# Finishing the last MLP product of a two-layer block in token blocks, with resident weights and a running final norm

## The chip, the cores and the metric

The program runs on all eight cores of one Trainium2 chip. The cores do the same work on different tokens and do not communicate. The time of a run is the device time of the slowest core, in microseconds (us). The program has a second, slower state in some executions: a run of the kernel before that took 1701.93 us is one of them. A ratio of two kernels is the mean time of one kernel's fast runs over that of the other's fast runs of the same rounds, so it is not quite the ratio of the medians.

Names: PE is the matmul engine (TensorE), PEld its weight loads, DVE is VectorE, ACT is ScalarE, POOL is GpSimd, SP is SyncE, which here only issues stores and waits. An engine with a "q" behind its name (SPq, POOLq) is its instruction sequencer.

## The reference, cut to what matters

The model is a two-layer block over latent tokens. Each layer mixes tokens and then applies a squared-ReLU MLP. The whole study is about the last two lines of work: the second MLP product of the second layer, and the final norm.

```python
def rmsnorm(x, g):
    xf = x.astype(jnp.float32)
    y = xf * lax.rsqrt(jnp.mean(xf * xf, axis=-1, keepdims=True) + EPS)
    return (y * g.astype(jnp.float32)).astype(x.dtype)

def sq_relu_mlp(h, w1, w2):
    return jnp.square(jax.nn.relu(h @ w1)) @ w2
# ... for each layer:
        x = x + g2 * sq_relu_mlp(h, mlp_w1[i], mlp_w2[i])
# ...
    return rmsnorm(x, final_g)
```

There are 16,384 latent tokens, 2,048 for each core. D_MODEL is 1024, so a token's output has eight chunks of 128 features; the hidden width is 4096. On the chip the features lie on the 128 partitions and the tokens along the free dimension.

## The kernel before

The tokens of a core are four tiles of 512. The MLP works on two tiles at once, so the last product covers the last 1,024 tokens. For each output chunk `fo`, 32 matmuls accumulate over the hidden features for each tile, then DVE adds the result to the residual:

```python
    def mlp_2(st):
        l, g = st["l"], st["g"]
        for fo in range(NCH):
            bks = [P.bank() for _ in st["pieces"]]
            for hf in range(2):
                w = w_take(("w2", l, g, 2 * fo + hf)).rearrange("p (a b) -> p a b", a=16)
                for ti, tile in enumerate(st["pieces"]):
                    # ... 16 matmuls of N = 512 columns into bks[ti]; after hf == 1:
                            P.stt(xv[:, fo, :], bk[:, o:o + n], MOD[:, l, 40 + fo, col:col + 1], xv[:, fo, :], ALU.mult, ALU.add)
```

The final norm needs the mean square over all eight chunks. It is a matmul with a matrix of 1/1024 over the squares (the statistics matmuls), then Ln and Exp on ACT; DVE multiplies each chunk by `final_g` and the factor, and each pair of chunks is stored:

```python
        def fin(c):
            P.stt(xv[:, c, :], xv[:, c, :], GVEC[:, 4, c:c + 1], rs, ALU.mult, ALU.mult)
            if c % 2 == 1:
                outs.append(P.dma("sp", d_out[:, c - 1:c + 1, t * 512:(t + 1) * 512], xv[:, c - 1:c + 1, :]))
        return [(lambda i=i: norm_sq(tiles[t], sqv(SQF, 512), i, 4)) for i in range(4)] + \
               [lambda: norm_stat(sqv(SQF, 512), 512, rs)] + [(lambda c=c: fin(c)) for c in range(NCH)]
    # ...
    run_all(mlp_2(l1[1]))
    for t in (2, 3):
        for f in fin_pieces(t):
            f()
    S.op("sp", None, extra_deps=outs)      # SP waits for all stores
```

All operations pass through a list scheduler in the program (class `Sched`), which fixes each engine's order before the kernel is built and derives the semaphore waits.

The softmax here doesn't subtract the row's maximum and nothing guards it: scores larger than these inputs give would overflow.

Of the kernel before, what the change touches and what calls it, by code (L numbers as in the profile page):

```python
# [13 lines left out]
NCH = 8  # L14
# [12 lines left out]


class _Op:
    __slots__ = ("id", "eng", "chan", "fn", "deps", "signal", "waits", "pos", "inc", "sigval", "cost", "mode", "unit", "prio")  # L30


class Sched:
# [7 lines left out]
    def __init__(self, nc):  # L41
        self.nc = nc
        self.ops = []
        self.streams = {k: [] for k in ("pe", "act", "dve", "pool", "sp")}
        self.chan_ops = {}
        self.buckets = {}
        self.base = {}
        self.hold, self.boost = None, 0

    def rects(self, ap):  # L50
        name = ap.tensor.name
# [63 lines left out]

    def op(self, eng, fn, reads=(), writes=(), chan=None, inc=1, extra_deps=(), cost=100.0, mode=None, join=False):
        o = _Op()
        o.cost, o.mode, o.prio = cost, mode, self.boost
        if self.hold is not None and eng == "pe":
            join = self.hold > 0  # L120
            self.hold += 1
        o.unit = join
        o.id = len(self.ops)
        o.eng = eng
        o.chan = chan or eng
        o.fn = fn
        o.inc = inc
        o.signal = chan is not None
        o.waits = []
        o.sigval = 0  # L130
        accs = []
        for ap in reads:
            if ap is None or isinstance(ap, (int, float)):
                continue
            sp, rs = self.rects(ap)
            for r in rs:
                accs.append((sp, r, sp == "ps"))
        for ap in writes:
            sp, rs = self.rects(ap)
            for r in rs:  # L140
                accs.append((sp, r, True))
        o.deps = self._query_insert(o, accs)
        for d in extra_deps:
            o.deps[d.id] = True
        self.ops.append(o)
        self.streams[eng].append(o)
        lst = self.chan_ops.setdefault(o.chan, [])
        lst.append(o)
        o.pos = len(lst)
        return o  # L150
# [22 lines left out]
    def reorder(self):  # L173
        ops = self.ops
        units = {e: [] for e in self.streams}
        unit_of = [None] * len(ops)
        for o in ops:
            lst = units[o.eng]
            if o.unit and lst:
                lst[-1].append(o)  # L180
            else:
                lst.append([o])
            unit_of[o.id] = (o.eng, len(lst) - 1)
        need, succ = {}, {}
        for e, lst in units.items():
            for i, u in enumerate(lst):
                ds = {unit_of[d] for o in u for d in o.deps}
                ds.discard((e, i))
                need[(e, i)] = len(ds)
                for d in ds:  # L190
                    succ.setdefault(d, []).append((e, i))
        end = [0.0] * len(ops)
        free = {e: 0.0 for e in units}
        head = {e: 0 for e in units}
        taken = {e: [False] * len(l) for e, l in units.items()}
        avail = {e: {} for e in units}
        best = {e: None for e in units}
        dma_free, mode = 0.0, None
        order = []

        def virtual(e, i):
            v, acc = 0.0, 0.0
            for o in units[e][i]:
                for d in o.deps:
                    if unit_of[d] != (e, i):
                        t = end[d] + (0.0 if ops[d].chan == e == "pe" else self.SEM) - acc
                        if t > v:
                            v = t
                acc += o.cost
            return v  # L210

        def pick(e):
            lim = head[e] + self.WINDOW[e]
            cand = []
            for i, v in avail[e].items():
                if i < lim:
                    s = max(free[e], v)
                    if e == "pe" and mode is not None and units[e][i][0].mode != mode:
                        s += 100.0
                    cand.append((s, i))  # L220
            if not cand:
                return None
            lo, li = min(cand)
            tol = lo + min(1500.0, max(150.0, 0.5 * sum(o.cost for o in units[e][li])))
            s, i = min(((s, i) for s, i in cand if s <= tol), key=lambda c: c[1] - units[e][c[1]][0].prio)
            return (s, i)

        for k, n in need.items():
            if n == 0:
                avail[k[0]][k[1]] = virtual(*k)  # L230
        left = len(need)
        while left:
            e, b = None, None
            for k in units:
                if best[k] is None and avail[k]:
                    best[k] = pick(k)
                if best[k] is not None and (b is None or best[k][0] < b[0]):
                    e, b = k, best[k]
            s, i = b
            t = s  # L240
            for o in units[e][i]:
                for d in o.deps:
                    if unit_of[d] != (e, i):
                        t = max(t, end[d] + (0.0 if ops[d].chan == e == "pe" else self.SEM))
                if o.chan.startswith("dma:"):
                    dma_free = max(dma_free, t + 0.6 * self.LAT) + o.cost
                    end[o.id] = dma_free + 0.4 * self.LAT
                    t += 540.0 if e == "pool" else 60.0
                else:
                    t += o.cost  # L250
                    end[o.id] = t + (90.0 if e == "pe" else 0.0)
                order.append(o)
            if e == "pe":
                mode = units[e][i][-1].mode
            free[e] = t
            taken[e][i] = True
            del avail[e][i]
            while head[e] < len(taken[e]) and taken[e][head[e]]:
                head[e] += 1
            best[e] = None  # L260
            left -= 1
            for k in succ.get((e, i), ()):
                need[k] -= 1
                if need[k] == 0:
                    avail[k[0]][k[1]] = virtual(*k)
                    best[k[0]] = None
        self.ops_in_order = order
        self.streams = {e: [o for o in order if o.eng == e] for e in self.streams}
        self.chan_ops = {}
        for o in order:  # L270
            lst = self.chan_ops.setdefault(o.chan, [])
            lst.append(o)
            o.pos = len(lst)
# [61 lines left out]
class Prog:  # L335
# [87 lines left out]
    def stt(self, out, in0, scalar, in1, op0, op1):  # L423
        return self.S.op("dve", lambda e: e.scalar_tensor_tensor(out, in0, scalar, in1, op0, op1),  # L424
                         reads=[in0, in1, scalar], writes=[out], cost=self.ew_cost("dve", "stt", out, [in0, in1]))

    def shuf(self, out, in_, mask):
        return self.S.op("dve", lambda e: e.stream_shuffle(out, in_, mask), reads=[in_], writes=[out],  # L428
                         cost=190.0 + 1.05 * self.n_of(out))
# [21 lines left out]
def run_all(gen):  # L451
    for _ in gen:
        pass
# [37 lines left out]
def build():  # L491
# [63 lines left out]
    def rot(key, lst):  # L555
        i = ctr.get(key, 0)
        ctr[key] = i + 1
        return lst[i % len(lst)]
# [52 lines left out]
    def w_take(key):  # L611
        ada_flush()
        while ada_take(ST):
            pass
        nxt = ST.items[ST.pos][0]
        if nxt[0] in extra:
            extra[nxt[0]](*nxt[1:])
        return ST.take(key)
# [7 lines left out]
    def plan_mlp(l, g, rounds1, rounds2, q0={}):  # L626
        ext1 = [("ada", l_, r_, c) for l_, r_ in rounds1 for c in range(4)]
        ext2 = [("ada", l_, r_, c) for l_, r_ in rounds2 for c in range(4)]
        for j in range(16):
            ST.add(("w1", l, g, j), d_w1[l, j])  # L630
            if j % 2 == 1 and ext1:
                k = ext1.pop(0)
                ST.add(k, d_ada[k[1], k[2], k[3]])
        for j in range(16):
            ST.add(("w2", l, g, j), d_w2[l, j // 2, j % 2])
            if j in q0:
                ST.add(("wq0", q0[j]), d_wq[q0[j]])
            if ext2 and j >= 1:
                k = ext2.pop(0)
                ST.add(k, d_ada[k[1], k[2], k[3]])  # L640
        assert not ext1 and not ext2
# [735 lines left out]
    run_all(mlp_a)  # L1377
    spread(mlp_2(l1[0]), st_norm(l1[1], 0) + st_norm(l1[1], 1))
    spread(mlp_1(l1[1]), fin_pieces(0) + fin_pieces(1), 2, 2)
    run_all(mlp_2(l1[1]))  # L1380
    for t in (2, 3):
        for f in fin_pieces(t):
            f()
    S.op("sp", None, extra_deps=outs)
    S.emit()
    return nc
# [116 lines left out]
```

## Time and profile before

| | before |
|---|---|
| fast runs | 1514.5 and 1516.05 us (the other two runs, 1701.93 and 1714.51 us, were slow) |
| spans of the cores in the profiled run | 1505.0 to 1514.3 us |
| PE busy in the slowest core | 1431.5 of 1514.3 us |
| last product, first to last matmul | 110.67 us on each core |
| from there to the last instruction (the tail) | 18.67 us, mean of cores (17.9 to 19.5) |

The first two lines below are of the page of the slowest core: its span, and each engine's busy time with its share of the span.

```profile
span 1514.3 us, 23295 instructions; the slowest of 8 cores (1505.0 to 1514.3 us)
...
PE 1431.5 (95%) x8436; PEld 694.0 (46%) x8436; DVE 600.9 (40%) x1003; ACT 583.2 (39%) x841; POOL 304.5 (20%) x371
```

PE is the bottleneck over the whole. The end is another matter. The next lines are of the timeline of the kernel before: start in us, duration, engine, line, operation, tiles written and read, shape, count of merged instructions, and in brackets the engine's idle time and what ended it. A merged row lasts from its first start to its last end.

```profile
1494.84 0.38 PE L387 MATMUL ps<-hid_175,ring_61 128*128 128x512 bf16 x1
...
1495.05 2.48 PE L387 MATMUL ps<-sqf_176,onesm_46 128*128 128x512 bf16 x10
...
1498.56 10.90 DVE L424 SCALAR_TENSOR_TENSOR xm_55<-xm_55,small_43,rs_63 128x512 f32<-128x512 f32 x16 [2.48 <-ACT rs_63 L397]
...
1500.04 9.86 SPq L447 DMA_DIRECT2D outT<-xm_55  x8
```

The last product matmul ends at 1495.22 us. Most statistics matmuls follow it. DVE's sixteen final multiplies begin at 1498.56 and run for 10.90 us in one row; the eight stores go out as they come. The chain of waits shows the same (start, duration, what; it is followed back from the end):

```profile
1449.89 47.07 PE ps L387 x218
...
1498.36 2.00 ACT sqf_176 L397 x2
...
1502.55 0.70 ACT rs_63 L397
...
1504.07 0.75 DVE xm_55 L424
...
1505.48 3.98 DVE xm_55 L424 x6
```

The end is one long row of DVE work behind a finished PE. Stores follow within a few us.

Two more lines are of the view of the source line that opens the program's block. At the end of the block each engine executes a DRAIN and then all meet at a barrier. The columns are duration min/median/max in ns, then the start of the first and last in us.

```profile
L311 POOLq DRAIN  x1: 8888/8888/8888, 1461.3 to 1461.3; - x1
...
L311 SPq DRAIN  x1: 7/7/7, 1514.1 to 1514.1; - x1
```

POOL's DRAIN takes 8.9 us here, but it begins at 1461.3, with POOL's last weight load, it is over at 1470.1, and nobody waits for it.

### The profile page before, as it was taken

Reading aid. Unit: us, or ns where it says so; the run is one execution under the profiler, and the core shown is the slowest. Engines: PE = TensorE matmul, PEld = TensorE weight load, DVE = VectorE, ACT = ScalarE, POOL = GpSimd, SP = SyncE. Lnnn points to the kernel's source line nnn. Section 1 sums busy time; section 2 is a strip of 40 time slices with the busy share of each in tenths; the row PEclk is TensorE's granted clock in tenths of the full one; section 3 lists DMA queues with packets and bytes.
Section 4 is the critical chain, followed back from the end, with each engine's and each line's share of the span. In section 5 each row is a group of like instructions: output and inputs, shape, how many; then the busy total and the mean of one; then the engine's idle time right before and its main releaser. Section 6 shows DMA issues by size and latency. Waiting matters only on the chain.

```text
span 1514.3 us, 23295 instructions; the slowest of 8 cores (1505.0 to 1514.3 us)
## 1 busy us (share of the span) xinstructions
PE 1431.5 (95%) x8436; PEld 694.0 (46%) x8436; DVE 600.9 (40%) x1003; ACT 583.2 (39%) x841; POOL 304.5 (20%) x371
## 2 busy tenths in 40 slices
PE   1699999999999999999997999899999999999996
PEld 0344445555555555555543334334444444444442
DVE  0177874443221344322248666443443222552003
ACT  2464363335110333323018778774334121432002
POOL 2025400010100010110135666552000000000000
PEclk9999999999999999999998999999999999999998
DMA  9554715545663455664354000400444444663432
GB/s 193 152 126 70 131 28 94 98 84 90 118 113 63 77 89 104 104 108 74 62 94 74 8 2 2 70 2 15 72 82 70 80 74 71 134 130 70 84 56 111
DMA packets 39808, 124.16 MB, mean 82 GB/s; under 512 B 4240, under 2 KB 4624, under 8 KB 39312
## 3 DMA queue, kind: packets, MB, share of 16 engines
q0 software_dynamic: 29504, 102.90, 39.9%
q1 hardware_dynamic: 10192, 19.76, 4.1%
q8 instruction: 70, 1.15, 0.3%
q14 instruction: 42, 0.34, 0.1%
HBM read 217.15 MB, written 8.39 MB: 149 GB/s over the span
## 4 chain that ended last, share of the span: by engine, by line
PE 90%; DMA 3%; DVE 2%; issue 2%; ACT 1%; POOL 1%; SPq 0%; DVEq 0%; ACTq 0%; POOLq 0%
PE ps L387 89%; DMA xm_55<-xT 2%; DMA ring_59<-ada_r 1%; DVE xm_55 L424 0%; SPq L447 0%; DVE tmp_65 L414 0%; ACT xb_68 L397 0%; POOL qt_122 L414 0%; ACT rs_63 L397 0%; DVE tb_129 L414 0%; DVE tb_130 L428 0%; DVE tb_127 L414 0%; POOL dt_75 L414 0%; DVE tb_128 L414 0%; DVE tb_130 L414 0%
## 5 line engine op out<-in xcount | busy, mean ns | idle before, releaser
L424 DVE SCALAR_TENSOR_TENSOR xm_55<-ps,mod_44,xm_55 128x512 f32<-128x512 f32 (+2 forms) x136 | 97.4, 718 | 296.4 <-PE ps L387 296.1
L397 ACT ACTIVATE tmp_64<-ps 128x512 f32<-128x512 f32 (+2 forms) x156 | 84.8, 543 | 213.6 <-PE ps L387 161.8
L397 ACT ACTIVATE tmp_65<-ps 128x512 f32<-128x512 f32 (+2 forms) x157 | 85.3, 544 | 159.5 <-PE ps L387 98.1
L397 ACT ACTIVATE sqf_176<-xm_55 128x1024 bf16<-128x1024 f32 x16 | 16.7, 1053 | 158.9 <-DVE xm_55 L424 156.9
L387 PE MATMUL ps<-xb_68,win_67 128*128 128x512 bf16 (+1 forms) x192 | 50.2, 422 | 10.2 <-ACT xb_68 L397 9.5
L387 PE MATMUL ps<-h_0_98,ring_61 128*128 128x408 bf16 (+3 forms) x336 | 58.9, 335 | 0.0
L387 PE MATMUL ps<-h_0_98,ring_58 128*128 128x384 bf16 (+3 forms) x336 | 58.9, 335 | 0.0
L414 DVE TENSOR_TENSOR tmp_64<-xm_55,rs_63 128x512 f32<-128x512 f32 (+2 forms) x44 | 33.8, 767 | 48.2 <-ACT rs_63 L397 41.9
L397 ACT ACTIVATE rs_63<-ps,epsv_51 128x512 f32<-128x512 f32 (+3 forms) x16 | 10.6, 666 | 105.2 <-PE ps L387 104.9
L387 PE MATMUL ps<-hid_99,ring_61 128*128 128x416 bf16 (+3 forms) x288 | 51.0, 335 | 0.0
L387 PE MATMUL ps<-h_0_98,ring_60 128*128 128x416 bf16 (+3 forms) x288 | 50.5, 335 | 0.0
L387 PE MATMUL ps<-h_0_98,ring_57 128*128 128x416 bf16 (+3 forms) x288 | 50.4, 335 | 0.0
L387 PE MATMUL ps<-h_0_98,ring_59 128*128 128x416 bf16 (+3 forms) x288 | 50.4, 335 | 0.0
L447 POOL DMA_DIRECT2D ring_59<-w_r x27 | 14.3, 531 | 171.8 <-PE ps L387 171.7
L414 DVE TENSOR_TENSOR hid_100<-tmp_64 128x416 bf16<-128x416 f32 (+3 forms) x48 | 27.9, 581 | 43.8 <-ACT tmp_64 L397 43.8
L414 DVE TENSOR_TENSOR hid_99<-tmp_64 128x416 bf16<-128x416 f32 (+3 forms) x48 | 27.9, 581 | 41.2 <-ACT tmp_64 L397 41.1
L387 PEld LDWEIGHTS ps<-h_0_98,ring_61 128*128 128x128 bf16 x336 | 32.5, 97 | 25.1 <-issue 0.6
L387 PEld LDWEIGHTS ps<-h_0_98,ring_58 128*128 128x128 bf16 x336 | 32.4, 98 | 25.0 <-issue 0.8
L447 POOL DMA_DIRECT2D ring_61<-w_r x27 | 14.3, 530 | 143.3 <-PE ps L387 143.1
L414 DVE TENSOR_TENSOR hid_99<-tmp_65 128x416 bf16<-128x416 f32 (+3 forms) x48 | 27.9, 581 | 37.7 <-ACT tmp_65 L397 37.7
L414 DVE TENSOR_TENSOR hid_100<-tmp_65 128x416 bf16<-128x416 f32 (+3 forms) x48 | 27.9, 581 | 36.0 <-ACT tmp_65 L397 36.0
L447 POOL DMA_DIRECT2D ring_60<-w_r x24 | 12.7, 530 | 138.4 <-PE ps L387 103.7
(803 smaller groups left out, 3136.9 us busy)
## 6 DMA issues: line engine op xcount, KB each, us to landing
ring_61<-w_r POOLq DMA_DIRECT2D x27, 512.0 KB, 5.7
ring_59<-w_r POOLq DMA_DIRECT2D x27, 512.0 KB, 5.8
ring_58<-w_r POOLq DMA_DIRECT2D x26, 512.0 KB, 5.8
ring_57<-w_r POOLq DMA_DIRECT2D x24, 512.0 KB, 5.8
ring_60<-w_r POOLq DMA_DIRECT2D x24, 512.0 KB, 5.9
outT<-xm_55 SPq DMA_DIRECT2D x16, 512.0 KB, 4.9
xm_55<-xT SPq DMA_DIRECT2D x6, 1024.0 KB, 9.0
ring_58<-ada_r POOLq DMA_DIRECT2D x12, 512.0 KB, 5.2
```

The source lines that it names most:

```text
L387: return self.S.op("pe", lambda e: e.matmul(out, lhsT, rhs, start=start, stop=stop), reads=[lhsT, rhs], writes=[out], cost=max(30.0 if hal ...
L397: return self.S.op("act", lambda e: e.activation(out, in_, func, bias=bias, scale=scale), reads=[in_, scale, bias], writes=[out], cost=175 ...
L414: return self.S.op(eng, lambda e: e.tensor_tensor(out, in0, in1, op), reads=[in0, in1], writes=[out], cost=self.ew_cost(eng, "tt", out, [i ...
L424: return self.S.op("dve", lambda e: e.scalar_tensor_tensor(out, in0, scalar, in1, op0, op1), reads=[in0, in1, scalar], writes=[out], cost= ...
L447: return self.S.op(q, lambda e: e.dma_start(out=out, in_=in_), reads=[in_], writes=[out], chan="dma:" + slot, inc=16, extra_deps=dep, cost ...
```

## The change

The intent: let most of the final norm, multiplies and stores run under matmuls. The first four output chunks are computed for all 1,024 tokens as before. The other four are computed for 768 tokens, and then, at the very end, for the last 256 tokens, with the eight weight pieces still resident. While PE does those last 128 matmuls, the other engines finish the 768 tokens. The squares go into the statistics chunk by chunk, so that the norm is ready soon after the last chunk. Two of the last block's eight multiplies go to POOL and ACT, and the stores alternate between the SP and ACT queues.

```diff
@@ plan_mlp
-            ST.add(("w2", l, g, j), d_w2[l, j // 2, j % 2])
+            if (l, g) != (1, 1) or j < 12:
+                ST.add(("w2", l, g, j), d_w2[l, j // 2, j % 2])
@@ the end of build()
-    run_all(mlp_2(l1[1]))
-    for t in (2, 3):
-        for f in fin_pieces(t):
-            f()
     ...
+    blocks = [(0, 0, 512, P.bk(7)[:, 0:512], RS[0][:, 0:512]), (1, 0, 256, P.bk(6)[:, 0:256], RS[1][:, 0:256]),
+              (1, 256, 512, P.bk(5)[:, 0:256], RS[1][:, 256:512])]
     ...
+    for j in range(12, 16):            # into buffers that are dead by now
+        w2_of[j] = HB[(j - 12) // 2][:, (j % 2) * 2048:(j % 2) * 2048 + 2048]
+        P.dma("pool", w2_of[j], d_w2[1, j // 2, j % 2], slot="w2l%d" % j)
     ...
+    def last_res(bk, ti, a, b, fo):
+        xv = tiles[2 + ti][0][0][:, fo, a:b]
+        P.stt(xv, bk[:, 0:b - a], MOD[:, 1, 40 + fo, 0:1], xv, ALU.mult, ALU.add)
+        sq = rot("sql", SQL)
+        P.act(sq[:, 0:b - a], xv, AF.Square)
+        for t_, a_, b_, sb, _ in blocks:
+            if t_ == ti and a <= a_ and b_ <= b:
+                P.mm(sb, ONESM, sq[:, a_ - a:b_ - a], start=(fo == 0), stop=(fo == NCH - 1))
+    def last_fin(k, c):
+        ti, a, b, sb, rs = blocks[k]
+        xv = tiles[2 + ti][0][0][:, c, a:b]
+        if k == 2 and c in (2, 5):
+            tmp = TMP[c % 2][:, 0:b - a]
+            P.tt(tmp, xv, rs, ALU.mult, eng="pool")
+            P.act(xv, tmp, AF.Copy, scale=GVEC[:, 4, c:c + 1])
+        else:
+            P.stt(xv, xv, GVEC[:, 4, c:c + 1], rs, ALU.mult, ALU.mult)
+        t0 = (2 + ti) * 512
+        outs.append(P.dma("sp" if c % 2 == 0 else "act", d_out[:, c, t0 + a:t0 + b], xv))
     ...  chunks 0 to 3 for both tiles; chunks 4 to 7 for blocks 0 and 1; rms_of blocks 0 and 1
+    for fo in range(4, NCH):
+        bk = P.bank()
+        for j in (2 * fo, 2 * fo + 1):
+            last_mm(bk, 1, 256, 512, j)
+        last_res(bk, 1, 256, 512, fo)
+        for c in (2 * fo - 8, 2 * fo - 7):
+            last_fin(0, c)
+        for c in (2 * fo - 8, 2 * fo - 7):
+            last_fin(1, c)
+    rms_of(blocks[2][3], 256, blocks[2][4])
+    for c in range(NCH):
+        last_fin(2, c)
```

The diff also adds a helper `addc` and a scheduler flag `pin`; neither is used.

More of the change, by code (lines that the diff above doesn't have):

```diff
@@ L29 @@
 class _Op:
-    __slots__ = ("id", "eng", "chan", "fn", "deps", "signal", "waits", "pos", "inc", "sigval", "cost", "mode", "unit", "prio")
+    __slots__ = ("id", "eng", "chan", "fn", "deps", "signal", "waits", "pos", "inc", "sigval", "cost", "mode", "unit", "prio", "pin")
 class Sched:
@@ L47, in __init__ @@
         self.base = {}
-        self.hold, self.boost = None, 0
+        self.hold, self.boost, self.pin = None, 0, False
     def rects(self, ap):
@@ L117, in op @@
         o = _Op()
-        o.cost, o.mode, o.prio = cost, mode, self.boost
+        o.cost, o.mode, o.prio, o.pin = cost, mode, self.boost, self.pin and eng == "pe"
         if self.hold is not None and eng == "pe":
@@ L212, in pick @@
         def pick(e):
-            lim = head[e] + self.WINDOW[e]
+            lim = head[e] + (1 if head[e] < len(units[e]) and units[e][head[e]][0].pin else self.WINDOW[e])
             cand = []
@@ L425, in stt, with addc @@
                          reads=[in0, in1, scalar], writes=[out], cost=self.ew_cost("dve", "stt", out, [in0, in1]))
+    def addc(self, out, in_):
+        return self.S.op("dve", lambda e: e.tensor_reduce(out, in_.rearrange("p c n -> p n c"), mybir.AxisListType.X, ALU.add),
+                         reads=[in_], writes=[out], cost=160.0 + 1.04 * self.n_of(in_))
     def shuf(self, out, in_, mask):
@@ L1379, in build @@
     spread(mlp_1(l1[1]), fin_pieces(0) + fin_pieces(1), 2, 2)
-    run_all(mlp_2(l1[1]))
-    for t in (2, 3):
-        for f in fin_pieces(t):
-            f()
+    P.ring, P.rr = list(range(5)), 0
+    SQL = [P.t("sql", E0 + i * 1024, [512], BF16) for i in range(4)]
+    blocks = [(0, 0, 512, P.bk(7)[:, 0:512], RS[0][:, 0:512]), (1, 0, 256, P.bk(6)[:, 0:256], RS[1][:, 0:256]),
+              (1, 256, 512, P.bk(5)[:, 0:256], RS[1][:, 256:512])]
+    last = l1[1]
+    w2_of = {}
+    for j in range(12, 16):
+        w2_of[j] = HB[(j - 12) // 2][:, (j % 2) * 2048:(j % 2) * 2048 + 2048]
+        P.dma("pool", w2_of[j], d_w2[1, j // 2, j % 2], slot="w2l%d" % j)
@@ new lines, in last_mm @@
+    def last_mm(bk, ti, a, b, j):
+        w = w2_of[j].rearrange("p (a b) -> p a b", a=16)
+        for h in range(16):
+            P.mm(bk[:, 0:b - a], w[:, h, :], last["HID"](ti, 16 * (j % 2) + h)[:, a:b],
+                 start=(j % 2 == 0 and h == 0), stop=(j % 2 == 1 and h == 15))
+    def last_res(bk, ti, a, b, fo):
[6 more added lines that the diff above has]
+                P.mm(sb, ONESM, sq[:, a_ - a:b_ - a], start=(fo == 0), stop=(fo == NCH - 1))
@@ new lines, in build @@
+    for fo in range(4):
+        bks = [P.bank(), P.bank()]
+        for j in (2 * fo, 2 * fo + 1):
+            w2_of[j] = w_take(("w2", 1, 1, j))
+            for ti in range(2):
+                last_mm(bks[ti], ti, 0, 512, j)
+            ST.free()
+        for ti in range(2):
+            last_res(bks[ti], ti, 0, 512, fo)
+    for fo in range(4, NCH):
+        for j in (2 * fo, 2 * fo + 1):
+            if j < 12:
+                w2_of[j] = w_take(("w2", 1, 1, j))
+        for ti, a, b, _, _ in blocks[0:2]:
+            bk = P.bank()
+            for j in (2 * fo, 2 * fo + 1):
+                last_mm(bk, ti, a, b, j)
+            last_res(bk, ti, a, b, fo)
@@ new lines, in build @@
+    for k in range(2):
+        rms_of(blocks[k][3], blocks[k][2] - blocks[k][1], blocks[k][4])
+    for fo in range(4, NCH):
+        bk = P.bank()
+        for j in (2 * fo, 2 * fo + 1):
+            last_mm(bk, 1, 256, 512, j)
[7 more added lines that the diff above has]
+        last_fin(2, c)
```

## The prediction

> **What bounds the kernel now.** PE: busy 1431.5 of 1514.3 us (page, part 1), 90% of the chain of waits. In the last MLP product (timeline from 1384.3 us) 128x512 matmuls start every 0.216 us until 1495.2 us, without a weight wait. PE work can't shrink there; the change adds to it. What can shrink is the tail, 1495.2 to 1514.3 us, 19.1 us, 1.3% of the span. That caps the gain below 2%.
>
> The tail before (timeline, chain of waits, slowest core): 16 statistics matmuls and two Ln/Exp pairs; DVE starts the final multiplies at 1498.6 and runs sixteen of 0.68 us without a gap to 1509.5 (10.9 us); eight 512 KB stores go out as they come, at about 375 GB/s (DMA view), bytes end near 1512; last landing 1514.3.
>
> **What the change does.** For 768 of these tokens the product ends about 14 us before PE does; their norm, multiplies and 3 MB of stores then run under the last 256 tokens' 128 matmuls.
>
> Costs on PE (on the critical path):
> - Statistics matmuls move before the last product's end: 8 x 0.216 + 15 x 0.11 = 3.4 us more there.
> - 256 matmuls of 256 columns replace 128 of 512: estimate 0.6 us, from a fixed 2.5 ns each. The Trainium skill, "TensorE: Matmul & The Clock Gate" (Part 1, the section on 56 against 53.3 ns), gives N/2.4 GHz plus about 2.5 ns; this trace agrees: 0.2155 us at 512 columns, about 0.056 at 128 (eight key/value matmuls in 0.61 us, the last one's 0.22 latency included), with 98 ns weight loads hidden.
> - Small stalls where a statistics matmul waits for Square: 0.5 us.
>
> PE therefore ends at about 1499.7 instead of 1495.2.
>
> Under the last 14 us: DVE 8 x 0.70 + 8 x 0.47 + 4 x 0.48 = about 11 us, starting some 2.5 us in; it fits barely. Stores 3 MB at 375 GB/s = 8.4 us; fit. Four resident weight loads go early into dead buffers; I expect no weight wait.
>
> New tail after PE's last product matmul (estimates for 256 columns from 128x256 forms in the groups): residual 0.6, Square 0.45, statistics matmul 0.35, Ln and Exp 1.1, six DVE multiplies 2.9 (the other two on POOL and ACT are parallel), last 128 KB store about 2.8 to landing: about 8.3 us. The skill's "DMA: Bandwidth & Descriptors" (Anatomy of one DMA) gives about 2 us fixed per DMA; this trace has 2.3 us from the last bytes to the end.
>
> End: 1499.7 + 8.3 = 1508.0 against 1514.3. The run's time was the span plus 1.5 us: about **1509.5 us**, range 1503 to 1515, against fast runs of 1514.5 and 1516.05: 0.4% faster. Chances: faster by over 2% 0.01, within 2% 0.98, slower by over 2% 0.01. Other stages keep their schedule.
>
> **Right if the profile shows:** PE's last 128x512/128x256 product matmul near 1499 to 1500; DVE and DMA busy in the 14 us before; only six DVE multiplies after; tail of 7 to 9 us from PE's end; DMA active to the end at a lower rate; mean granted clock unchanged.
>
> **Wrong if:** DVE, delayed by its late start, carries multiplies of the first blocks beyond PE's end, or PE's order puts statistics matmuls before their Square (idle PE with releaser ACT), or ACT, which now also issues stores, waits in order for DVE and delays Square; each costs 1 to 4 us. PE gaps at 256 columns over 0.115 us would cost more. Or the slower state falls in most of the runs.

## The result

Four runs of the kernel after took 1513.7, 1513.19, 1514.01 and 1510.93 us, median 1513.45. The ratio of fast runs to those of the kernel before is 0.9985, 95% interval 0.9961 to 1.0009: the same within 2%, and not clear of zero. Timed again later, in five rounds (run e9 below), the ratio was 0.9970, interval 0.9957 to 0.9983.

Such a small step is better read from the trace. The slowest core decides the time, and on each core the last product starts somewhere between 1374 and 1389 us, differently in each execution, before the change as after it. From the start of the last product on, a core is almost the same in every execution. This table is worked out from the traces of all eight cores: "product" is from the first to the modelled end of the last matmul of the last product, "tail" is from there to the core's last instruction, "stage" is the sum (means of the cores).

| | product | tail | stage |
|---|---|---|---|
| before | 110.67 | 18.67 (17.9 to 19.5) | 129.33 |
| after | 114.24 | 12.08 (12.08 to 12.09) | 126.33 |
| predicted change | +4.5 | -10.8 | -6.3 |
| measured change | +3.57 | -6.59 | -3.00 |

The change gains 3.0 us, half of what I forecast. And one thing catches the eye: before, the tails differ by 1.6 us between cores, because the landing of the last stores does; after, all eight cores agree within 0.01 us. Something of a fixed length ends the program after the change.

The page after, the same lines as before:

```profile
span 1512.1 us, 23658 instructions; the slowest of 8 cores (1502.9 to 1512.1 us)
...
PE 1428.2 (94%) x8572; PEld 706.8 (47%) x8572; DVE 603.0 (40%) x1013; ACT 586.0 (39%) x857; POOL 306.1 (20%) x373
```

The timeline after, for the slowest core (its last product matmul ends at 1499.98):

```profile
1498.10 9.23 SPq L452 DMA_DIRECT2D outT<-xm_55  x5
...
1499.71 0.27 PE L387 MATMUL ps<-hid_175,h_136 128*128 128x256 bf16 x1
...
1501.23 0.27 PE L387 MATMUL ps<-sql_180,onesm_46 128*128 128x256 bf16 x1 [1.14 <-ACT sql_180 L397]
...
1502.16 0.42 ACT L397 ACTIVATE rs_63<-rs_63 128x256 f32<-128x256 f32 x1
1502.68 3.49 DVE L424 SCALAR_TENSOR_TENSOR xm_55<-xm_55,small_43,rs_63 128x256 f32<-128x256 f32 x6 [2.10 <-ACT rs_63 L397]
1502.73 0.72 POOL L414 TENSOR_TENSOR tmp_64<-xm_55,rs_63 128x256 f32<-128x256 f32 x1 [66.10 <-ACT rs_63 L397]
1503.41 0.90 POOL L414 TENSOR_TENSOR tmp_65<-xm_55,rs_63 128x256 f32<-128x256 f32 x1
...
1505.11 0.51 ACT L397 ACTIVATE xm_55<-tmp_64,small_43 128x256 f32<-128x256 f32 x1 [2.53 <-DVE xm_55 L424]
...
1506.20 0.89 ACTq L452 DMA_DIRECT2D outT<-xm_55  x2
```

DVE begins its last multiplies 2.7 us after the product and is finished at 1506.17; the first two overlap with POOL's two. SP's last store is issued by 1507.33. Yet the span ends at 1512.1. The waits of SP over the end of the program (waiter, awaited, us in total, times, longest):

```profile
SPq L322 <- DVE xm_55 L424: 12.3, 7, 5.3
SPq L311 <- PEq L311: 2.1, 1, 2.1
SPq L322 <- ACT xm_55 L397: 1.5, 1, 1.5
SPq L322 <- DMA outT<-xm_55: 0.9, 1, 0.9
```

SP waits 0.9 us for the last store, and then 2.1 us more at line 311, the block's end, for something that this view calls PE's sequencer. PE had long been done, so it was another. The view of line 311 names it:

```profile
L311 POOLq EVENT_SEMAPHORE  x2: 17/17/17, 1511.9 to 1512.0; - x2
...
L311 POOLq DRAIN  x1: 9101/9101/9101, 1502.7 to 1502.7; - x1
...
L311 SPq DRAIN  x1: 7/7/7, 1509.9 to 1509.9; - x1
```

SP has seen all stores land at 1509.9. POOL's DRAIN starts at 1502.73 together with POOL's multiplies and takes 9.10 us, to 1511.83. Then the barrier opens (the POOLq events at 1511.9 and 1512.0). The chain of waits doesn't show this: it ends at DVE's multiplies, because drains are not counted as work there.

### The profile page after: what moved, and what is told of

Its sections match the earlier page's. It is cut to its first block, busy times and chain, and to the rows that moved or that the text cites. A ratio compares the mean times of both kernels' runs of the same rounds, so it can differ in the third digit from the quotient of the medians.

```text
span 1512.1 us, 23658 instructions; the slowest of 8 cores (1502.9 to 1512.1 us)
## 1 busy us (share of the span) xinstructions
PE 1428.2 (94%) x8572; PEld 706.8 (47%) x8572; DVE 603.0 (40%) x1013; ACT 586.0 (39%) x857; POOL 306.1 (20%) x373
## 3 DMA queue, kind: packets, MB, share of 16 engines
q8 instruction: 71, 1.16, 0.3%
## 4 chain that ended last, share of the span: by engine, by line
PE 90%; DMA 3%; DVE 2%; issue 2%; POOL 1%; ACT 1%; SPq 0%; DVEq 0%; ACTq 0%; POOLq 0%
PE ps L387 90%; DMA xm_55<-xT 2%; DMA ring_59<-ada_r 1%; SPq L452 0%; DVE tmp_65 L414 0%; ACT xb_68 L397 0%; DVE xm_55 L424 0%; POOL qt_122 L414 0%; POOL dt_75 L414 0%; DVE tb_129 L414 0%; DVE tb_130 L433 0%; ACT rs_63 L397 0%; DVE tb_127 L414 0%; DVE tb_128 L414 0%; DVE tb_130 L414 0%
## 5 line engine op out<-in xcount | busy, mean ns | idle before, releaser
L424 DVE SCALAR_TENSOR_TENSOR xm_55<-ps,mod_44,xm_55 128x512 f32<-128x512 f32 (+3 forms) x140 | 98.2, 704 | 289.3 <-PE ps L387 289.0
L397 ACT ACTIVATE rs_63<-ps,epsv_51 128x512 f32<-128x512 f32 (+4 forms) x17 | 10.9, 639 | 108.7 <-PE ps L387 108.4
L452 POOL DMA_DIRECT2D ring_59<-w_r x26 | 13.8, 531 | 165.4 <-PE ps L387 165.3
L387 PEld LDWEIGHTS ps<-h_0_98,ring_61 128*128 128x128 bf16 x336 | 32.5, 97 | 25.1 <-issue 0.6
L387 PEld LDWEIGHTS ps<-h_0_98,ring_58 128*128 128x128 bf16 x336 | 32.4, 98 | 25.0 <-issue 0.8
L452 POOL DMA_DIRECT2D ring_61<-w_r x26 | 13.8, 531 | 135.9 <-PE ps L387 135.7
L387 PEld LDWEIGHTS ps<-hid_99,ring_61 128*128 128x128 bf16 x288 | 27.9, 98 | 21.6 <-issue 0.6
L387 PEld LDWEIGHTS ps<-h_0_98,ring_57 128*128 128x128 bf16 x288 | 27.9, 97 | 21.6 <-issue 0.4
```

Of the source, the lines that this page charges most:

```text
L387: return self.S.op("pe", lambda e: e.matmul(out, lhsT, rhs, start=start, stop=stop), reads=[lhsT, rhs], writes=[out], cost=max(30.0 if hal ...
L397: return self.S.op("act", lambda e: e.activation(out, in_, func, bias=bias, scale=scale), reads=[in_, scale, bias], writes=[out], cost=175 ...
L424: return self.S.op("dve", lambda e: e.scalar_tensor_tensor(out, in0, scalar, in1, op0, op1), reads=[in0, in1, scalar], writes=[out], cost= ...
L452: return self.S.op(q, lambda e: e.dma_start(out=out, in_=in_), reads=[in_], writes=[out], chan="dma:" + slot, inc=16, extra_deps=dep, cost ...
```

## The experiments

**Theory A**: POOL's late work sets the end, since its exit DRAIN lasts some 9 us after POOL is used. The rest of the missing gain comes from what POOL's two multiplies do to DVE and to the order of the stores. **Rival B**: the end is set by the small stores and their latency; the drain only happens to end near them. **Rival C**: the gain was lost on PE, in statistics matmuls, narrow matmuls and stalls. Eleven runs were made; all gave correct results. e1, e9 and e10 were timed in several rounds. The others had one profiled execution each, so they are read by their stages alone. The runs were spread over three chips; the product of the kernel before was again 110.67 us in e4, and that of the kernel after 114.25 us in e9.

### e1: all multiplies on DVE

```diff
-        if k == 2 and c in (2, 5):
+        if False:
```

> All eight final multiplies of the last 256 tokens on DVE, none on POOL. In the kernel after, POOL's exit DRAIN starts with its late multiply and takes 9.10 us, ending 2.0 us after the last store landed (1511.83 against 1509.8). Theory A (POOL's late work sets the end): the tail from the last product matmul to the end falls from 12.08 us to 8.5 to 9.3 us on every core, DVE multiplies return to 0.47 us each (first two took 1.04 and 0.94), the product stays 114.2 us; time about 1510. Rival B (the end is set by the small stores' latency, POOL's drain only happens to end near it): the tail stays above 11 us.

Measured: product 114.24, tail 9.11 (8.70 to 9.74), stage 123.36 us. In three rounds the ratio to before is 0.9959, interval 0.9935 to 0.9983 (fast runs of this kernel 1508.46 to 1509.6). Line 311 and DVE's last multiplies in this kernel:

```profile
L311 POOLq EVENT_SEMAPHORE  x2: 17/17/17, 1507.4 to 1507.4; - x2
L311 POOLq DRAIN  x1: 8861/8861/8861, 1434.9 to 1434.9; - x1
...
L311 SPq DRAIN  x1: 7/7/7, 1507.3 to 1507.3; - x1
```

```profile
1501.55 3.25 DVE L424 SCALAR_TENSOR_TENSOR xm<-xm,small,rs 128x256 f32<-128x256 f32 x8 [2.11 <-ACT rs L397]
```

The drain is back where it hurts nobody, the barrier opens 0.1 us after SP, and the cores' tails differ again by the landing of their stores. Eight multiplies on DVE take 3.25 us; with two of them given to POOL, the other six took 3.49. So the help of POOL gained nothing even before its drain is counted. B falls: the stores are as small as before, and the tail is 9.11 us, not above 11. Theory A fits, but this run also lets the stores go out earlier; e3 separates the two.

### e2: POOL's multiplies moved to the block before

```diff
-        if k == 2 and c in (2, 5):
+        if k == 1 and c in (2, 5):
```

> The two POOL multiplies are moved from the last 256 tokens to the block before, so POOL still works, but some 9 us before the last product matmul. Theory A: POOL's drain is over before the last store lands, and the tail is 8.5 to 9.3 us, as with all multiplies on DVE. Rival C (any POOL work in this stage lengthens the end): the tail stays near 12 us.

Measured: tail 8.99, stage 123.24 us. Line 311, and DVE's row while POOL multiplies:

```profile
L311 POOLq EVENT_SEMAPHORE  x2: 17/17/17, 1509.5 to 1509.6; - x2
L311 POOLq DRAIN  x1: 9104/9104/9104, 1491.9 to 1491.9; - x1
```

```profile
1491.82 2.58 DVE L424 SCALAR_TENSOR_TENSOR xm<-xm,small,rs 128x256 f32<-128x256 f32 x3 [0.32 <-ACT rs L397]
```

POOL's use is not the harm, its lateness is: the same drain of 9.10 us now ends at 1501.0, under the tail. The three DVE multiplies that meet POOL's two take 2.58 us, where three alone would take about 1.3 (0.48 us for the last, 0.40 from start to start); here DVE has the time. (The "Rival C" of this expectation is not the one above; the tail of 8.99 us rules it out.)

### e3: one tiny late POOL operation

```diff
     rms_of(blocks[2][3], 256, blocks[2][4])
+    P.tt(TMP[0][:, 0:8], RS[1][:, 256:264], RS[1][:, 256:264], ALU.mult, eng="pool")
```

(on top of e1)

> As the first run, plus one POOL operation on 8 columns whose result nobody uses, after the last Exp. Theory A: POOL's drain takes about 9 us again whatever the size of the operation, the end is at Exp's end plus 9.3 us, tail 11.7 to 12.2 us, while DVE and the stores end as early as in the first run. If the 9 us were the work of the two real multiplies, the tail would be as in the first run (under 9.5 us).

Measured: tail 10.68 on every core, stage 124.93 us. Line 311, and POOL's operation:

```profile
L311 POOLq EVENT_SEMAPHORE  x2: 17/17/17, 1510.0 to 1510.1; - x2
...
L311 POOLq DRAIN  x1: 7734/7734/7734, 1502.2 to 1502.2; - x1
...
L311 SPq DRAIN  x1: 7/7/7, 1508.1 to 1508.1; - x1
```

```profile
1502.23 0.20 POOL L414 TENSOR_TENSOR tmp<-rs 128x8 f32<-128x8 f32 x1 [66.10 <-ACT rs L397]
```

An operation of 0.20 us on 8 columns, with a result nobody reads, costs 1.57 us over e1. My number was too high by 1 us or more, and that sharpens the theory: the drain is not 9 us from its start, it ends 7.5 us after the end of POOL's last operation. Here 1502.43 to 1509.94; in the kernel after 1504.31 to 1511.83. A DRAIN starts while its engine's last operations are still queued, so its length alone says little. DVE's ends 0.05 us after DVE's last operation in all profiles, ACT's within 0.2 us; only POOL's is late.

### e4: the same in the kernel before

```diff
     for t in (2, 3):
         for f in fin_pieces(t):
             f()
+    last = tiles[3][0][0][:, 7, 0:8]
+    P.tt(TMP[0][:, 0:8], last, last, ALU.mult, eng="pool")
```

> The kernel before, plus one POOL operation on 8 columns after the last final multiply, result unused. Before, POOL's drain is hidden (it ends near 1470). Theory A: the drain now begins at the end of DVE's work and lasts about 9 us, so the tail grows from 18.7 us (mean of cores) to 14.2 + 9.3 = about 23.5 us on every core, with the same DVE and store times. If the drain belongs to something that only the changed kernel has, the tail stays near 18.7 us.

Measured: product 110.67, tail 22.32 on every core (mean before: 18.67), stage 132.99 us. Line 311:

```profile
L311 POOLq EVENT_SEMAPHORE  x2: 17/17/17, 1516.0 to 1516.1; - x2
...
L311 POOLq DRAIN  x1: 7734/7734/7734, 1508.3 to 1508.3; - x1
L311 SPq DRAIN  x1: 7/7/7, 1512.4 to 1512.4; - x1
```

The 7.5 us rule gives 22.1 us for the end of the drain and 0.2 more for the barrier; the expectation was again too high, by 1.2 us. The mechanism has nothing to do with the change: a late POOL operation of 0.2 us makes the kernel before 3.7 us longer.

### e5: the running norm alone

All chunks for both tiles in order with streamed weights, running statistics, and nothing deferred; multiplies on DVE.

```diff
-    for fo in range(4):
+    for fo in range(NCH):
 ...
-    for fo in range(4, NCH):         # and all that follows
+    for k in range(3):
+        rms_of(blocks[k][3], blocks[k][2] - blocks[k][1], blocks[k][4])
+    for k in range(3):
+        for c in range(NCH):
+            last_fin(k, c)
```

> One part alone: the running statistics of the norm, with no output chunk deferred (all chunks for both tiles in order, streamed weights, all final multiplies on DVE after the product). If the deferral is what gains and the running norm only moves statistics matmuls onto the product: the product grows from 110.67 to about 114.1 us, the tail shrinks only from 18.7 to about 17.3 us (DVE's 1024 tokens of multiplies, 11.9 us, stay behind the product), so the stage is about 131.4 us, some 2 us longer than before's 129.3 us. If the running norm by itself gains, the stage is under 129 us.

Measured: product 113.71, tail 17.96, stage 131.67 us. DVE after the product:

```profile
1499.11 0.75 DVE L424 SCALAR_TENSOR_TENSOR xm<-ps,mod,xm 128x512 f32<-128x512 f32 x1 [2.70 <-PE ps L387]
1501.20 11.72 DVE L424 SCALAR_TENSOR_TENSOR xm<-xm,small,rs 128x512 f32<-128x512 f32 x24 [1.34 <-ACT rs L397]
```

DVE still has 11.72 us of multiplies behind the product. Without the deferral the new form loses 2.3 us: 3.04 us more on PE, 0.71 us less in the tail. This is not the running norm alone, in spite of the heading: the multiplies are also cut into three blocks (24 instead of 16, 11.72 us against 10.90), and the stores alternate between SP and ACT. The deferral on top of it (e1) gains 8.3 us: it is what the change lives from. The product lengths also give PE's costs. In the trace a statistics matmul takes 0.216 us of PE at 512 columns and 0.109 at 256. Seven chunks of these are within the product here, 7 x (0.216 + 2 x 0.109) = 3.04 us, which is all that the product grew (113.71 - 110.67). In the kernel after, those of the first two blocks' last chunk are within it too, 3.36 us in sum; that leaves 0.21 us of its 3.57 for the narrower product matmuls: 128 more of them at 2.5 ns are 0.32 us, and the last one's modelled end comes 0.11 us sooner after its start (0.27 against 0.38 us).

### e6: squares summed on DVE

On top of e1, DVE sums the squares of chunks 0 to 6, and a block gets two statistics matmuls instead of eight.

```diff
+        if fo == 0:
+            sq_of[ti] = sq
+        elif fo < NCH - 1:
+            prev = sq_of[ti][:, a:b] if fo == 1 else ACC[ti][:, a:b]
+            dst = ACB if fo == NCH - 2 else ACC
+            P.tt(dst[ti][:, a:b], prev, sq[:, 0:b - a], ALU.add)
 ...
-                P.mm(sb, ONESM, sq[:, a_ - a:b_ - a], start=(fo == 0), stop=(fo == NCH - 1))
+                if fo == NCH - 2:
+                    P.mm(sb, ONESM, ACB[ti][:, a_:b_], start=True, stop=False)
+                elif fo == NCH - 1:
+                    P.mm(sb, ONESM, sq[:, a_ - a:b_ - a], start=False, stop=True)
```

> As the run with all final multiplies on DVE, but the squares of the first seven chunks are summed on DVE, so each block needs two statistics matmuls instead of eight. Statistics matmuls on PE fall from about 3.4 us to 0.9 us of the product. If the 3.57 us by which the product grew are these matmuls plus 0.6 us for narrower product matmuls: product about 111.7 us, tail unchanged at 9.1 us, stage about 120.8 us instead of 123.4. If the growth is mainly due to stalls or narrower matmuls, the product stays above 113 us.

Measured: product 111.64 as expected, tail 9.66, stage 121.30 us. The product is 0.97 us longer than before's: the same arithmetic gives 0.76 us for the statistics matmuls that are left within it, and 0.21 us for narrower ones. So PE's growth has no stalls in it, and rival C is right about 3.57 us that were forecast (as 4.5) and wrong about the missing gain. The tail is 0.55 us longer than in e1: the last residual starts 0.48 us after the product instead of 0.11, and the last stores take 0.18 us more to land. The residual on the slowest core, where the product ends at 1495.44:

```profile
1495.92 0.48 DVE L424 SCALAR_TENSOR_TENSOR xm<-ps,mod,xm 128x256 f32<-128x256 f32 x1 [0.62 <-PE ps L387]
```

DVE is not busy with an earlier block then: it has sat idle for 0.62 us, and the trace of each core has its wait for PE ending 0.06 us after the product, 0.42 us before the residual starts. What held it is not shown.

### e7: block by block, with a last block of 128 tokens

On top of e1. The last four chunks are done block after block (512, 384, 128 tokens), each with its own chunks 4 to 7.

```diff
+    for k, (ti, a, b, sb, rs) in enumerate(blocks):
+        for fo in range(4, NCH):
+            bk = P.bank()
+            for j in (2 * fo, 2 * fo + 1):
+                last_mm(bk, ti, a, b, j)
+            last_res(bk, ti, a, b, fo)
+            if k > 0:
+                for c in (2 * fo - 8, 2 * fo - 7):
+                    last_fin(k - 1, c)
+        rms_of(sb, b - a, rs)
```

> As the run with all final multiplies on DVE, but the second half of the chunks goes block by block (512, 384, then the last 128 tokens), so less is left at the end: chain of the norm about 2.1 us instead of 2.6, eight multiplies of 128 columns at about 0.27 us instead of 0.40. Tail about 7.2 to 8.0 us instead of 9.1, product about 114.5 us (the narrower matmuls cost 2.5 ns more each, if 128 columns still hide their weight loads). If DVE is overrun by the multiplies of the 384 tokens, which have only some 7 us, the tail stays at 9 us or more.

Measured: product 114.40, tail 7.53, stage 121.93 us, as expected. The product is only 0.16 us longer than e1's, so even 128 columns hide their weight loads: the matmuls of 128 columns start 56 ns apart in the trace.

### e8: both

> The two changes of the last two runs together: product about 112 us, tail 7.2 to 8.0 us, stage about 119.5 us against 129.3 before and 126.3 after; time about 1505 if the stages before start as they did. If the added sums on DVE collide with the multiplies of 384 tokens, the tail grows by 1 us or more over the run before.

Measured: product 111.75, tail 8.74, stage 120.48 us. The collision I named happened. DVE near the end of the product (which ends at 1498.94 on this core):

```profile
1499.20 0.29 DVE L414 TENSOR_TENSOR acb<-acc,sql 128x128 bf16<-128x128 f32 x1
1499.61 0.62 DVE L424 SCALAR_TENSOR_TENSOR xm<-xm,small,rs 128x384 f32<-128x384 f32 x1
1500.15 0.35 DVE L424 SCALAR_TENSOR_TENSOR xm<-ps,mod,xm 128x128 f32<-128x128 f32 x1
```

The residual of the last chunk (the third row, reading `ps`) starts 1.2 us after its matmuls, behind a multiply of an earlier block. DVE takes its instructions in the order fixed when the program was built, so late side work stands in front of the critical step.

### e9, e10, e11: the kernel after again, and two versions that beat both

e9 is the kernel after, unchanged. e10 and e11 combine e1, e6 and e7, but stop the sums of the last block at chunk 3, so that its last steps don't pass through DVE; the last block has 192 tokens in e10 and 128 in e11. The diff is against e8, cut to the condition.

```diff
-                if fo == NCH - 2:
+                upto = 3 if k_ == 2 else NCH - 2
+                if fo == upto:
                     P.mm(sb, ONESM, ACB[ti][:, a_:b_], start=True, stop=False)
-                elif fo == NCH - 1:
-                    P.mm(sb, ONESM, sq[:, a_ - a:b_ - a], start=False, stop=True)
+                elif fo > upto:
+                    P.mm(sb, ONESM, s_, start=False, stop=(fo == NCH - 1))
```

> The kernel after, unchanged, timed again beside the kernel before and beside the best version on one chip: stage 126.3 us against 129.3, so about 3.0 us (0.2%) faster than before; ratio about 0.998.

> Best version: no late POOL work, squares of the chunks summed on DVE (for the last block only the first four chunks), blocks of 512, 320 and 192 tokens one after another. Product about 111.8 us, tail about 7.9 us (norm chain 2.4, eight multiplies at 0.33, issue 0.4, landing 2.2, exit 0.3), stage about 119.7 us against 129.3 before; about 9.6 us (0.6%) faster than before, ratio about 0.994.

> The same with a last block of 128 tokens. With the sums for the last block taken off DVE, the last residual no longer waits behind multiplies: product about 111.9 us, tail about 7.5 us as in the run with blocks alone (8.7 when all sums were on DVE), stage about 119.4 us.

| | product | tail | stage | time, fast runs | ratio to before (95%) |
|---|---|---|---|---|---|
| before, same rounds | 110.67 | 18.67 | 129.33 | 1514.28 to 1519.64 | 1 |
| e9, after | 114.25 | 12.08 | 126.33 | 1510.8 to 1513.85 | 0.9970 (0.9957 to 0.9983) |
| e10 | 111.94 | 8.36 | 120.30 | 1507.18 to 1508.89 | 0.9943 (0.9929 to 0.9957) |
| e11 | 111.96 | 7.53 | 119.49 | 1509.28, one run | |

(The stage of before is that of its profiled run above.) e10 is faster than before by 0.6%: the same by the measure of 2%, but clear of zero. Its interval ends where that of e9 begins (0.9957), and its fast runs are all below those of e9; two of its six runs were slow (1570.79 and 1663.98 us) and are left out. Its tail is 0.46 us longer than I expected. There too the last residual starts late, 0.46 us after the product instead of 0.11, though DVE's previous operation ended 1.7 us before the product did; the cause is open. In e11 it starts at 0.11 us, so not all of e11's shorter tail is owed to its smaller block. e11 has the shortest stage; it had one look only, and its time of one run is no evidence against the trace or for it.

## Why the prediction was right or wrong

**Right: what bounds the end, and the cap.** The gain could not reach 2%, since the whole tail is 1.3% of the span. The tail before was DVE's 1,024 tokens of multiplies, and deferring 256 tokens hides three quarters of them: e5 without the deferral keeps 11.72 us of multiplies and a tail of 17.96 us.

**Right within 1 us: the cost on PE.** Forecast +4.5 us, measured +3.57: 3.36 for statistics matmuls (I had 3.4), 0.21 net for narrower matmuls (I had 0.6), and none of the 0.5 I put down for stalls. The 0.6 was a wrong count: I charged the fixed 2.5 ns to all 256 narrow matmuls, though only 128 were added, which makes 0.3. The 2.5 ns of the Trainium skill's page (named in the prediction) themselves agree: in the trace the starts of product matmuls are 215.8 ns apart at 512 columns and 109.2 at 256, so two narrow ones take about 2.5 ns more than a wide one.

**Right: DVE fits under the last 14 us.** Its last multiply of the first two blocks ends at 1498.42 us, 1.6 us before the product.

**Wrong: the new tail, 8.3 us against 12.08.** The step that failed is "six DVE multiplies after" the norm "(the other two on POOL and ACT are parallel)", followed by the store "to landing" as the end. I treated POOL as free help. The terms, from the end of the product on:

| term | forecast | after | e1, no late POOL |
|---|---|---|---|
| residual to Exp, start of multiplies | 2.5 | 2.7 | 2.7 |
| last multiplies | 2.9 | 3.49 | 3.25 |
| end of DVE's work to last store issued | in the next term | 1.16 | 0.42 |
| issue to last landing | 2.8 | 2.44 | 2.45 |
| last landing to end of program | 0 | 2.28 | 0.29 |
| sum | about 8.3 | 12.08 | 9.11 |

(The measured columns are means of the eight cores; the rows add up within rounding.) Of the 3.8 us too much in the tail, 3.0 us go away when POOL's two multiplies go to DVE. Along SP's path, about 2.0 us of these are the wait for POOL's DRAIN behind the last landing (2.28 against 0.29). About 0.7 us are stores issued late: ACT's copy of POOL's result stood in ACT's order behind a store that waited for DVE (the 2.53 us in its row), SP waited 1.5 us for that copy, and the stores of chunks whose data were ready stood behind it. I had named ACT waiting in order for DVE as a danger, though for Square, not for the stores. About 0.2 us are DVE itself: its two multiplies beside POOL took 1.04 and 0.94 us instead of 0.48, so that six took longer than eight.

These three parts are not three costs that could be saved one by one, because in the kernel after POOL alone sets the end. Its first multiply starts 2.75 us after the product, the two take 1.58 us, the DRAIN ends 7.53 us after them, and the exit takes 0.23 us: in sum the 12.08 us, within rounding. Stores and DVE on time, with POOL unchanged, would not have moved it. Without the wait for the DRAIN, but with the late stores, the tail would be about 10.1 us, an estimate from the table (12.08 - 2.28 + 0.29).

**Mis-sized: the rest, 0.8 us.** It is e1's tail against the forecast. In e1, 0.29 us of the end are the exit after landing, which I had left out; the norm's chain was 0.2 us longer than forecast, and the eight multiplies 0.35 us longer than the six of the forecast. Issue and landing together, 2.87 us, were near my 2.8, but the reason I gave was a misreading: in the profile of before most of the stores' packets end near 1512.4, but one stream of 2 KB packets goes on to 1513.68, so that the last bytes lie 0.6 us before the end and not 2.3.

The stage as a whole missed by 3.3 us: 4.2 in the tail's change, less 0.9 that PE cost less than forecast. Of the 4.2, 3.8 are the new tail; the other 0.4 are the old one, for which I took the slowest core (19.1) where the mean is 18.67. That PE's error hid part of the tail's is luck.

**The time.** 1509.5 us was forecast and the median of after was 1513.45. Without POOL's part (e1) the median of the three fast runs is 1509.1 (the fourth was slow); spans vary by some us from execution to execution, so the stage and not this match is the evidence.

**Left open.** Why POOL's DRAIN takes 7.5 us after its last operation is not shown; neither the size (8 or 256 columns) nor the kernel matters. Why the last product's start differs by up to 12 us between cores in each execution was not studied. The profiled executions can't say how much each of the late stores and the drain would cost without the other, since in the kernel after the drain ends later than the stores and hides them; e3 shows the drain without the late stores (10.68).

## What to carry to other kernels

Before giving a late operation to an idle engine, look at what happens at the end of the program on that engine: here POOL's last operation had to lie some 7.5 us before the end, and one that came later lengthened the kernel whatever its size. An end that is equal on all cores to 0.01 us, where stores land differently, is the sign of a fixed wait, and it is found in the view of the line that closes the program, not in the chain of waits. Deferring the last tokens' matmuls behind resident weights did pay: with DVE left to finish the norm alone and summing squares, and with smaller last blocks, the last stage went from 129.3 to 120.3 us.

## What the Trainium skill lacked or had wrong

- "VectorE: DVE Perf Modes", section "The DRAIN you can't avoid", tells two kinds of DRAIN apart: VectorE's own after each operation, and boilerplate of about 12 ns from the preamble and postamble, on all five engines. The DRAIN at the end of this program's block, which carries the program's line 311, is not described there: it took 7 ns on SP, 0.1 to 0.6 us on ACT, 0.2 to 1.0 us on PE, 2.0 to 5.2 us on DVE (mostly DVE's own queued work) and 7.7 to 10.6 us on POOL, over all kernels and cores. POOL's ended 7.5 us beyond the end of a last compute operation, or 8.2 to 10.1 us beyond the issue of a last weight load. No page I read gives this cost of late POOL work.
- "GPSIMD Engine Reference", section "Specifications", says that POOL shares its SBUF interfaces with VectorE, with contention for DVE instructions with two SBUF inputs. It gives no size there; the runs agree and give one: a multiply of 128x256 with two SBUF inputs took 1.04 and 0.94 us beside POOL's multiply, 0.48 us without.
- "DMA: Bandwidth & Descriptors", section "Anatomy of one DMA", has about 2 us fixed per DMA, measured for DMAs that GpSimd issues. I found no such sum there for DMAs issued by SP and ACT, as the stores here are: at best 1.7 us from issue to landing for 128 KB, and e1's last ones landed 2.45 us, on the mean, after the end of their issue. Open as well: the first store that ACT issued held its sequencer for 2.05 to 2.47 us in the kernel after, e1, e2, e3, e6 and e9, but 0.37 to 0.38 us in e7, e8, e10 and e11. No run was made to find out why.
